# Differences of the inner activations stored with the MLPs' first products, and a list schedule ranked by due times

## The chip, the cores and the metric

The kernel runs on one core of one Trainium2 chip. A core has a matrix engine (TensorE, PE in the profile; PEld is its weight load), VectorE (DVE), ScalarE (ACT), GpSimd (POOL) and SyncE (SP). Here SP issues every DMA. Each engine works through its own instructions in the order in which they were written down, and waits on semaphores of the others. The metric is the device time of one execution in microseconds (us), the median of three runs.

## The reference

Two layers over 1024 tokens of width 1024 in f32, each a mixer and then an MLP:

```
for layer in range(2):
    h = rmsnorm(x, mix_norm[layer])
    x = x + (sliding_window_attention(h) if layer == 0 else hgrn2_recurrence(h))
    h = rmsnorm(x, mlp_norm[layer])
    x = x + square(relu(h @ w_up[layer])) @ w_down[layer]       # inner width 4096
return rmsnorm(x, final_norm)
```

The attention has 16 query heads, 4 key heads, a window of 128 and a sink in the softmax. The recurrence has 8 heads of 128 and chunks of 64, with a forget gate.

## The kernel before

**Tiles.** A tile is 128 features by 512 tokens (`TH`) of f32; two halves of the tokens make `hf` 0 and 1. A product in f32 precision is three matmuls in a faster format (`mm3`): a tile is split into a rounded part and a rest (`split` for activations, `weight_split` for weights), one cast on ACT or DVE and one subtraction on DVE. Tile names show their pool: `wr` raw weights, `wh` and `wl` their two parts, `m` sums of weights, `a` long-lived tiles, `t` short-lived ones, `p` and `q` banks of PSUM, `d` tensors in DRAM. Slots: 60 `a`, 18 `t`, 7 `m`, 5 each of `wr`, `wh`, `wl`, 4 each of `p` and `q`.

**Seven products.** The large matrix products use Strassen's scheme in Winograd's form, once: with the inputs halved in both directions, seven products numbered 1 to 7 take the place of eight. Their operands are the four quarters or sums of them. For activations with quarters 00, 01, 10, 11 (inner half, token half) product 1 takes 00, 2 takes 10, 3 takes 11, 5 takes 01 - 00, 6 takes 11 - (01 - 00), 7 takes 11 - 01, and 4 takes 10 - (11 - (01 - 00)).

**The MLP's first products.** `mlp` first makes the operands of the normalised x (`begin` for the first token half, `finish` for the second, both with splits) and the sums of squares (`weigh`), then calls `pair` for 16 pairs of inner tiles (m and m + 16). A pair runs its seven products of 12 matmuls each into two `q` banks and a `p` bank, reads the banks out, adds, and applies square(relu) to get the four quarters of the inner activations (`square_relu`). `keep` stores each of the four to DRAM by a DMA.

**The MLP's second products.** `down` goes over the 16 inner tiles in passes: products 1 and 5 together, then 6, 7, 4, 2 and 3. For each inner tile `operands` loads the quarters of the weights and of the inner activations that the product needs, makes the sum or difference (`sum_of`, DVE), and splits. The differences of products 5, 6 and 4 build on each other: they live in 16 `a` tiles `T[p]` from pass to pass, and likewise the weights' sums in `S[p]`. Eight activation loads are issued for each inner tile: one for product 1 (its quarter also serves 5), one more for 5, one for 6, two for 7, and one each for 4, 2 and 3.

**The HGRN layer.** `hgrn_constants` makes the lower bounds of the forget gate (small operations on 128 x 8) and the masks (integer operations on 128 x 64). Then `finish` makes the operands of x, `two_first` starts the first head, and eight heads follow: `gates` (Strassen products by `two`) interleaved with the `recurrence` of the head before. `final` makes the last norm.

**What sets the order.** The code above doesn't issue instructions. `Schedule.add` (line 149) notes each operation with its engine or engines, a cost in ns, and what it depends on. `Schedule.order` (line 183) then runs a list schedule: on the engine that is free earliest it takes, of the operations that are ready by its model, the one of the lowest rank, and never idles while one is ready. `LATENCY` is the model's time between engines. A DMA costs its bytes over 320 an ns, at least 650 ns, and lands 2000 ns later. The slots of a pool are given out in the order of the program. The rank is the operation's number in the program less a lead:

```
op.rank = (len(self.ops) - lead, len(self.ops))
```

The lead is 100 operations for the loads and splits of weights (`LEAD`) and for whatever reads a `p` bank (`EVACUATE`), -200 for the last outputs, otherwise 0. Casts can go to ACT or DVE; `better_elsewhere` decides by what is queued. `issue` (line 273) writes the instructions in that order, from one line (341), which is why nearly every row of the profile names L341 and groups are told apart by tiles.

Of the kernel before, what the change touches and what calls it, by code (L numbers as in the profile page):

```python
# [14 lines left out]
ALU = mybir.AluOpType  # L15
AX = mybir.AxisListType

P = 128
T = 1024
# [3 lines left out]
TH = T // NH  # L23
FF = 4096
MT = FF // P
# [93 lines left out]


class Op:
    __slots__ = ("ways", "tail", "bufs", "first", "wait", "ready", "after", "rank", "engine", "form")


ENGINES = ("SP", "PE", "ACT", "DVE", "Pool")
# [7 lines left out]
WEIGH = 1.0  # L133
DRAIN = {"whole": 120.0, "columns": 120.0}
LEAD = 100
EVACUATE = 100
HK = KT // 2


class Schedule:  # L140
# [8 lines left out]
    def add(self, ways, outs, ins, tail=0.0, form=None):  # L149

        op = Op()
        op.ways, op.tail, op.engine, op.form = ways, tail, None, form
        lead = self.lead
        if any(isinstance(v, View) and v.buf.tag == "p" for v in ins):
            lead = max(lead, EVACUATE)
        op.rank, op.ready, op.after, op.first = (len(self.ops) - lead, len(self.ops)), 0.0, [], []
        before, bufs = set(), {}  # L160
        for views, writes in ((ins, False), (outs, True)):
            for v in views:
                if isinstance(v, View):
                    bufs[v.buf] = None
                    before.update(v.buf.conflicts(v.part, writes))
        for views, writes in ((ins, False), (outs, True)):
            for v in views:
                if isinstance(v, View):
                    v.buf.note(op, v.part, writes)
        before.discard(op)  # L170
        op.bufs = list(bufs)
        for b in op.bufs:
            if b.uses == 0:
                op.first.append(b)
                self.tags.setdefault((id(b.pool), b.tag), []).append(b)
            b.uses += 1
            b.users.append(op)
        op.wait = len(before) + len(op.bufs)
        for o in before:
            o.after.append(op)  # L180
        self.ops.append(op)

    def order(self):
        free_at, pending, ready, done, form = {}, {}, {}, [], None
        slots, queue = {}, {}
        for key, bufs in self.tags.items():
# [10 lines left out]
        def give(key):  # L197
            while queue[key] and slots[key]:
                b = queue[key].pop()
                t, b.slot = heapq.heappop(slots[key])  # L200
                for op in b.users:
                    met(op, t)
# [4 lines left out]
                    heapq.heappush(pending.setdefault(e, []), (0.0, op.rank, op))  # L207
        for key in self.tags:
            give(key)
        def better_elsewhere(op, e, t):  # L210
            waiting = sum(o.ways[e][1] for _, o in ready[e] if not o.engine and len(o.ways) == 1)
            for other, (_, cost) in op.ways.items():
                if other != e:
                    ahead = sum(o.ways[other][1] for r, o in ready.get(other, ()) if r < op.rank and not o.engine)
                    if max(t, free_at.get(other, 0.0)) + ahead + cost < t + op.ways[e][1] + WEIGH * waiting:
                        return True
            return False

# [74 lines left out]
class Net:  # L293
# [32 lines left out]
    def a(self, dt=F32, shape=(P, TH)):  # L326
        return self.tile("a", BUFS["a"], shape, dt)
# [171 lines left out]
        return h, self.token_rstd(self.sum_squares([self.x[kt][hf] for kt in range(KT)]))  # L499


    def square_relu(self, m, hf, c, psum):

        r = self.t()
        if psum:
            c, h = straight(c), halves(r)
            self.act(h, c, AF.Relu)
            self.stt(h, c, 0.0, h, ALU.max, ALU.mult)
        else:
            self.stt(r, c, 0.0, c, ALU.max, ALU.mult)  # L510
        self.hid[m, hf] = self.keep(r)

    def gained(self, which, kt, hf):

# [91 lines left out]
    def pair(self, m, x):  # L606

        w = self.strassen_weights(*(self.io["up"][self.layer, i] for i in (m, m + MT // 2)))

        def read(ps):  # L610
            z = self.t()
            self.take(z, ps)
            return z

        main, side, own = self.psum("q"), self.psum("q"), self.psum()
        self.product(main, w[1], x[1], True)
        u1 = read(main)
        self.product(own, w[2], x[2], True)
        self.product(side, w[5], x[5], True)
        p5 = read(side)  # L620
        self.product(main, w[6], x[6], False)
        u2 = read(main)
        self.product(side, w[3], x[3], False)
        self.product(main, w[7], x[7], False)
        u3 = read(main)
        self.product(main, w[4], x[4], False)
        self.add_bank(u1, own)
        self.square_relu(m, 0, u1, False)
        self.add_bank(u2, side)
        self.square_relu(m, 1, u2, False)  # L630
        self.tt("any", p5, p5, u3, ALU.add)
        self.square_relu(m + MT // 2, 1, p5, False)
        self.square_relu(m + MT // 2, 0, main, True)

    def mlp(self, cut):

        x = self.mlp_second()
        for m in range(MT // 2):
            if m == MT // 2 - 2:
                self.r = [self.a() for _ in range(NH)]  # L640
                for hf in range(NH):
                    self.copy(self.r[hf], self.spread(self.square[hf]))
            self.pair(m, x)
        yield from self.down(cut)

    def hidden(self, i, hf, p):
        z = self.t()
        self.dma(z, self.hid[p + i * MT // 2, hf], 4 * P * TH)
        return z

    def operands(self, name, p, T, S, held=False):

        a = lambda i, k: self.raw(self.io["down"][self.layer, k, p, :, i])
        h = lambda i, hf: self.hidden(i, hf, p)

        def sum_of(tile, x, y, alu=ALU.subtract):
            self.tt("any", tile, x, y, alu)
            return tile

        if name == 1:  # L660
            self.corner = a(0, 0), h(0, 0)
            w, x = self.corner
        elif name == 5:
            first, q00 = self.corner
            T[p] = x = sum_of(self.a(), h(0, 1), q00)
            w = sum_of(self.t(tag="m"), a(1, 0), a(1, 1), ALU.add)
        elif name == 6:
            T[p] = x = sum_of(T[p], h(1, 1), T[p])
            w = S[p]
        elif name == 7:  # L670
            x = sum_of(self.t(), h(1, 1), h(0, 1))
            w = sum_of(self.t(tag="m"), a(0, 0), a(1, 0))
        elif name == 4:
            x = sum_of(T[p], h(1, 0), T[p])
            w = a(1, 1)
        elif name == 2:
            w, x = a(0, 1), h(1, 0)
        else:
            x = h(1, 1)
            w = sum_of(S[p], a(0, 1), S[p])  # L680
        got = self.split(w) if held else self.weight_split(w), self.split(x)
        if name == 5:
            S[p] = sum_of(self.a(), w, first)
        return got

    def down(self, cut):
# [2 lines left out]


        n, ahead = MT // 2, 2
        T, S, y = {}, {}, {}
        main = [self.psum("q") for _ in range(HK)]
        side = [self.psum() for m in range(HK)]

# [11 lines left out]
        def run_pass(names, held=0):  # L707
            ws, todo = {}, list(range(n))
            for p in range(n):
                while todo and todo[0] <= p + ahead or (todo and todo[0] >= n - held and p >= n - held - 1):  # L710
                    q = todo.pop(0)
                    for name in names:
                        ws[name, q] = self.operands(name, q, T, S, q >= n - held)
                if p < n - held:
                    products(names, [p], ws, True, n - held - 1)
            return ws
# [551 lines left out]
        self.spill(0)  # L1268

    def hgrn(self, layer):  # L1270
        self.hgrn_constants()
        x, r = self.finish(layer, True), [self.a() for _ in range(NH)]
        begun = [self.two_first(which, 0, x) for which in ((0, 3), (1, 2))]
        self.rs.append(self.token_rstd(self.sum_squares([self.x[kt][1] for kt in range(KT)]), keep=True))
        for y, z in zip(r, self.rs):
            self.copy(y, self.spread(z))
        self.spill(1)
        ys, totals = [[], []], []
        before = iter(())
        for e in range(KT):  # L1280
            got = []
            interleave(self.gates(e, x, self.rs, r, got, [None] * 2 if e else begun), before, 14, 10)
            before = self.recurrence(e, got, totals, ys)
        run(before)
        for y in ys:
            y[:-1] = [self.take_back(kept) for kept in y[:-1]]
        self.hgrn_out(0, ys[0], totals[0])
        self.mlp_first(layer)
        self.hgrn_out(1, ys[1], totals[1])
# [120 lines left out]
```

## Time and profile before

| | us |
|---|---|
| three runs | 2086.87, 2078.36, 2085.83 |
| median | 2085.83 |
| profiled execution, its time | 2076.22 |
| its span, first to last instruction | 2074.4 |
| TensorE busy | 2009.9 |
| VectorE busy | 1809.3 |
| ScalarE busy | 841.8 |
| mean granted TensorE clock | 0.987 of full |

In the order of the span, by the chain of waits and the tiles in use: attention and its projections to about 330 us; the first layer's `pair` products to about 622, its passes of `down` to about 911; the HGRN layer to about 1460; the second layer's pairs to about 1760 and its passes to 2054; the last norm to the end. DMA traffic is heaviest in the passes of `down`.

A row of a group gives the engine, the operation, output and input tiles, the shape and the count; then busy time, mean ns of one, and the engine's idle time just before them with what ended it. A row of the timeline gives the start, the length, the instruction and in brackets the idle time before it with what ended it. A row of a table of stretches gives for each engine its busy time and the number of its instructions, then the granted clock, the share of the DMA engines and GB/s.

### The profile page before, as it was taken

Reading aid. Unit: us, or ns where it says so; the run is one execution under the profiler, and the core shown is the slowest. Engines: PE = TensorE matmul, PEld = TensorE weight load, DVE = VectorE, ACT = ScalarE, POOL = GpSimd, SP = SyncE. Lnnn points to the kernel's source line nnn. Section 1 sums busy time; section 2 is a strip of 40 time slices with the busy share of each in tenths; the row PEclk is TensorE's granted clock in tenths of the full one; section 3 lists DMA queues with packets and bytes.
Section 4 is the critical chain, followed back from the end, with each engine's and each line's share of the span. In section 5 each row is a group of like instructions: output and inputs, shape, how many; then the busy total and the mean of one; then the engine's idle time right before and its main releaser. Section 6 shows DMA issues by size and latency. Waiting matters only on the chain.

```text
span 2074.4 us, 32285 instructions
## 1 busy us (share of the span) xinstructions
PE 2009.9 (97%) x11374; PEld 1722.8 (83%) x11374; DVE 1809.3 (87%) x3598; ACT 841.8 (41%) x1767; POOL 63.8 (3%) x124
## 2 busy tenths in 40 slices
PE   7999999999999999979999999999999999999996
PEld 6878778888888888868888888878788888888886
DVE  8899899777789998899999999879977778999887
ACT  5567765112134334564333333333511124433442
POOL 4030000000000000000100000000000000000001
PEclk9999999999999999999999999999999999999998
DMA  6212363333368877722111111547333337887652
GB/s 209 87 47 81 114 204 126 116 112 122 117 226 291 290 238 251 262 97 72 62 62 57 62 57 62 194 138 243 112 115 116 116 122 237 294 276 241 221 173 82
DMA packets 176450, 316.49 MB, mean 153 GB/s; under 512 B 19744, under 2 KB 23840, under 8 KB 176288
## 3 DMA queue, kind: packets, MB, share of 16 engines
q1 hardware_dynamic: 176288, 314.43, 46.7%
q8 instruction: 89, 1.46, 0.3%
q14 instruction: 73, 0.60, 0.1%
HBM read 250.39 MB, written 63.96 MB: 152 GB/s over the span
## 4 chain that ended last, share of the span: by engine, by line
PE 77%; DVE 14%; DMA 3%; ACT 3%; issue 2%; SPq 0%; DVEq 0%; ACTq 0%
PE q L341 44%; PE p L341 33%; DVE a L341 6%; DVE t L341 4%; DVE m L341 2%; DVE wl L341 2%; DMA wr<-in_down 2%; ACT t L341 1%; ACT a L341 1%; DMA a<-in_x 0%; DMA t<-d 0%; DVE sm L341 0%; DMA t<-in_x 0%; DMA a<-d 0%; ACT wh L341 0%
## 5 line engine op out<-in xcount | busy, mean ns | idle before, releaser
L341 PE MATMUL q<-a,wh 128*128 128x512 f32 x2560 | 763.1, 381 | 10.1 <-ACT t L341 5.9
L341 PE MATMUL p<-a,wh 128*128 128x512 f32 x2336 | 721.4, 388 | 12.9 <-ACT wh L341 11.2
L341 PEld LDWEIGHTS q<-a,wh 128*128 128x128 f32 x2560 | 485.5, 190 | 83.8 <-ACT t L341 8.3
L341 PEld LDWEIGHTS p<-a,wh 128*128 128x128 f32 x2336 | 436.1, 191 | 76.9 <-ACT wh L341 12.0
L341 PE MATMUL q<-a,wl 128*128 128x512 f32 x1280 | 483.1, 381 | 0.3 <-DVE wl L341 0.3
L341 PE MATMUL p<-a,wl 128*128 128x512 f32 x1168 | 447.8, 384 | 0.0
L341 PEld LDWEIGHTS q<-a,wl 128*128 128x128 f32 x1280 | 243.2, 190 | 35.5 <-DVE wl L341 0.7
L341 DVE TENSOR_TENSOR wl<-wr,wh 128x512 fp32r<-128x512 f32 x352 | 240.8, 685 | 11.1 <-ACT wh L341 2.1
L341 PEld LDWEIGHTS p<-a,wl 128*128 128x128 f32 x1168 | 222.7, 191 | 32.6 <-issue 1.2
L341 ACT COPY t<-q 128x512 f32<-128x512 f32 (+2 forms) x201 | 111.5, 561 | 318.0 <-PE q L341 313.4
L341 DVE TENSOR_TENSOR a<-t,a 128x512 fp32r<-128x512 f32 (+1 forms) x294 | 194.9, 683 | 3.6 <-DMA t<-d 3.5
L341 DVE TENSOR_TENSOR wl<-m,wh 128x512 fp32r<-128x512 f32 x256 | 175.0, 685 | 8.2 <-ACT wh L341 1.3
L341 ACT CAST a<-t 128x512 fp32r<-128x512 f32 x198 | 119.5, 617 | 118.7 <-PE q L341 47.5
L341 DVE TENSOR_TENSOR t<-t,t 128x512 f32<-128x512 f32 (+3 forms) x268 | 161.9, 624 | 5.8 <-ACT t L341 2.7
L341 ACT CAST wh<-wr 128x512 fp32r<-128x512 f32 x153 | 94.0, 618 | 160.3 <-PE p L341 89.7
L341 DVE CAST wh<-wr 128x512 fp32r<-128x512 f32 x199 | 85.2, 428 | 81.4 <-PE p L341 51.7
L341 ACT CAST wh<-m 128x512 fp32r<-128x512 f32 x145 | 89.7, 620 | 144.1 <-PE q L341 80.8
L341 DVE TENSOR_TENSOR m<-wr,wr 128x512 f32<-128x512 f32 x160 | 109.6, 686 | 34.9 <-DMA wr<-in_up 18.0
L341 PE MATMUL p<-wh,a 128*128 128x512 f32 x384 | 121.8, 389 | 10.1 <-ACT a L341 8.3
L341 PEld LDWEIGHTS q<-t,t 128*64 128x64 f32 (+1 forms) x2160 | 98.0, 144 | 24.4 <-issue 11.3
L341 PE MATMUL q<-t,t 128*64 128x32 f32 (+2 forms) x2160 | 111.6, 230 | 0.4
L341 ACT CAST a<-a 128x512 fp32r<-128x512 f32 x111 | 67.7, 620 | 79.5 <-DVE a L341 39.5
(117 smaller groups left out, 2082.7 us busy)
## 6 DMA issues: line engine op xcount, KB each, us to landing
t<-d SPq DMA_DIRECT2D x296, 256.0 KB, 4.7
wr<-in_down SPq DMA_DIRECT2D x256, 256.0 KB, 4.0
d<-t SPq DMA_DIRECT2D x180, 256.0 KB, 2.9
wr<-in_up SPq DMA_DIRECT2D x128, 256.0 KB, 2.9
wr<-in_win SPq DMA_DIRECT2D x68, 256.0 KB, 2.8
a<-d SPq DMA_DIRECT2D x60, 256.0 KB, 4.2
wr<-in_wqkv SPq DMA_DIRECT2D x48, 256.0 KB, 2.9
d<-a SPq DMA_DIRECT2D x48, 256.0 KB, 2.5
```

Source lines behind the costliest of these rows:

```text
L341: fn(*[place(a) for a in args], **{k: place(v) for k, v in kw.items()})
```

## The change

Three things change.

The differences of the inner activations are made in `pair` and stored there: seven tensors for each pair instead of four, named by the product that takes them. `operands` loads the one tensor that its product needs, so `T` and its 16 tiles are gone, and the loads for an inner tile go from eight to seven.

`hgrn_constants` is called in the first layer's `mlp`, ahead of its pair 1, instead of at the start of `hgrn`.

The rank becomes a time. `due` first gives every operation a `now`: the TensorE time of all matmuls ahead of it in the program. Then, from the last operation to the first, an operation is due so early that everything that follows from it can still be in time: a matmul at its `now`, any other at most `SLACK` (10 us) after its own `now`. The lead counts as `STEP` (120 ns) each, so 100 are 12 us. `better_elsewhere` now adds, for the other engine too, what is ready there and can run nowhere else.

```diff
@@ class Schedule
+SLACK = 10000.0
+STEP = 120.0
...
-        op.rank, op.ready, op.after, op.first = (len(self.ops) - lead, len(self.ops)), 0.0, [], []
+        op.rank, op.ready, op.after, op.first = lead, 0.0, [], []
...
+    def due(self):
+
+        clock, now = 0.0, []
+        for op in self.ops:
+            now.append(clock)
+            if "PE" in op.ways:
+                clock += op.ways["PE"][1]
+        for i in reversed(range(len(self.ops))):
+            op = self.ops[i]
+            cost = min(c for _, c in op.ways.values())
+            late = now[i] + SLACK
+            for o in op.after:
+                late = min(late, o.due - max(LATENCY[e][w] for e in op.ways for w in o.ways))
+            if "PE" in op.ways:
+                late = min(late, now[i])
+            op.due = late - cost - op.tail
+            op.rank = ((now[i] if "PE" in op.ways else op.due) - STEP * op.rank, i)
+
     def order(self):
+        self.due()
...
+        def load(e):
+            return sum(o.ways[e][1] for _, o in ready.get(e, ()) if not o.engine and len(o.ways) == 1)
+
         def better_elsewhere(op, e, t):
-            waiting = sum(o.ways[e][1] for _, o in ready[e] if not o.engine and len(o.ways) == 1)
+            here = t + op.ways[e][1] + WEIGH * load(e)
...
-                    if max(t, free_at.get(other, 0.0)) + ahead + cost < t + op.ways[e][1] + WEIGH * waiting:
+                    if max(t, free_at.get(other, 0.0)) + ahead + cost + WEIGH * load(other) < here:
@@ pair
+        def kept(name, z):
+            self.hid[name, m] = self.keep(z)
+
         self.add_bank(u1, own)
-        self.square_relu(m, 0, u1, False)
+        h00 = self.square_relu(u1)
+        kept(1, h00)
         self.add_bank(u2, side)
-        self.square_relu(m, 1, u2, False)
+        h01, t5, t6, t4 = self.square_relu(u2), *(self.t() for _ in range(3))
+        self.tt("any", t5, h01, h00, ALU.subtract)
+        kept(5, t5)
         self.tt("any", p5, p5, u3, ALU.add)
-        self.square_relu(m + MT // 2, 1, p5, False)
-        self.square_relu(m + MT // 2, 0, main, True)
+        h11 = self.square_relu(p5)
+        kept(3, h11)
+        self.tt("any", t6, h11, t5, ALU.subtract)
+        kept(6, t6)
+        self.tt("any", h01, h11, h01, ALU.subtract)
+        kept(7, h01)
+        h10 = self.square_relu(main, True)
+        kept(2, h10)
+        self.tt("any", t4, h10, t6, ALU.subtract)
+        kept(4, t4)
@@ mlp
+            if m == 1 and self.layer == 0:
+                self.hgrn_constants()
             self.pair(m, x)
@@ operands
-            self.corner = a(0, 0), h(0, 0)
-            w, x = self.corner
+            w = self.corner = a(0, 0)
         elif name == 5:
-            first, q00 = self.corner
-            T[p] = x = sum_of(self.a(), h(0, 1), q00)
             w = sum_of(self.t(tag="m"), a(1, 0), a(1, 1), ALU.add)
         elif name == 6:
-            T[p] = x = sum_of(T[p], h(1, 1), T[p])
             w = S[p]
         elif name == 7:
-            x = sum_of(self.t(), h(1, 1), h(0, 1))
             w = sum_of(self.t(tag="m"), a(0, 0), a(1, 0))
         elif name == 4:
-            x = sum_of(T[p], h(1, 0), T[p])
             w = a(1, 1)
...
-        got = self.split(w) if held else self.weight_split(w), self.split(x)
+        got = self.split(w) if held else self.weight_split(w), self.split(self.hidden(name, p))
@@ hgrn
-        self.hgrn_constants()
```

More of the change, by code (lines that the diff above doesn't have):

```diff
@@ L121 @@
 class Op:
-    __slots__ = ("ways", "tail", "bufs", "first", "wait", "ready", "after", "rank", "engine", "form")
+    __slots__ = ("ways", "tail", "bufs", "first", "wait", "ready", "after", "rank", "engine", "form", "due")
 ENGINES = ("SP", "PE", "ACT", "DVE", "Pool")
@@ L499, in scaled, with square_relu @@
         return h, self.token_rstd(self.sum_squares([self.x[kt][hf] for kt in range(KT)]))
-    def square_relu(self, m, hf, c, psum):
+    def square_relu(self, c, psum=False):
         r = self.t()
@@ L510, in square_relu @@
             self.stt(r, c, 0.0, c, ALU.max, ALU.mult)
-        self.hid[m, hf] = self.keep(r)
+        return r
     def gained(self, which, kt, hf):
@@ L642, in mlp, with hidden, operands @@
                     self.copy(self.r[hf], self.spread(self.square[hf]))
+            if m == 1 and self.layer == 0:
+                self.hgrn_constants()
             self.pair(m, x)
         yield from self.down(cut)
-    def hidden(self, i, hf, p):
+    def hidden(self, name, p):
         z = self.t()
-        self.dma(z, self.hid[p + i * MT // 2, hf], 4 * P * TH)
+        self.dma(z, self.hid[name, p], 4 * P * TH)
         return z
-    def operands(self, name, p, T, S, held=False):
+    def operands(self, name, p, S, held=False):
         a = lambda i, k: self.raw(self.io["down"][self.layer, k, p, :, i])
-        h = lambda i, hf: self.hidden(i, hf, p)
         def sum_of(tile, x, y, alu=ALU.subtract):
@@ L660, in operands @@
         if name == 1:
-            self.corner = a(0, 0), h(0, 0)
-            w, x = self.corner
+            w = self.corner = a(0, 0)
         elif name == 5:
-            first, q00 = self.corner
-            T[p] = x = sum_of(self.a(), h(0, 1), q00)
             w = sum_of(self.t(tag="m"), a(1, 0), a(1, 1), ALU.add)
         elif name == 6:
-            T[p] = x = sum_of(T[p], h(1, 1), T[p])
             w = S[p]
         elif name == 7:
-            x = sum_of(self.t(), h(1, 1), h(0, 1))
             w = sum_of(self.t(tag="m"), a(0, 0), a(1, 0))
         elif name == 4:
-            x = sum_of(T[p], h(1, 0), T[p])
             w = a(1, 1)
         elif name == 2:
-            w, x = a(0, 1), h(1, 0)
+            w = a(0, 1)
         else:
-            x = h(1, 1)
             w = sum_of(S[p], a(0, 1), S[p])
-        got = self.split(w) if held else self.weight_split(w), self.split(x)
+        got = self.split(w) if held else self.weight_split(w), self.split(self.hidden(name, p))
         if name == 5:
-            S[p] = sum_of(self.a(), w, first)
+            S[p] = sum_of(self.a(), w, self.corner)
         return got
@@ L691, in down @@
         n, ahead = MT // 2, 2
-        T, S, y = {}, {}, {}
+        S, y = {}, {}
         main = [self.psum("q") for _ in range(HK)]
@@ L712, in run_pass @@
                     for name in names:
-                        ws[name, q] = self.operands(name, q, T, S, q >= n - held)
+                        ws[name, q] = self.operands(name, q, S, q >= n - held)
                 if p < n - held:
```

## The prediction

> **What bounds the kernel now.** I read the page first, then the table of stretches, then TensorE's own timeline for its stalls, then the chain of waits around each. The profiled execution took 2076.22 us for a span of 2074.4, so 1.8 lies around the span; it is 9.6 us below the median of the three runs (2085.83). The sum is made against 2076.22 and the same difference is then taken off the median.
>
> ```profile
> span 2074.4 us, 32285 instructions
> PE 2009.9 (97%) x11374; PEld 1722.8 (83%) x11374; DVE 1809.3 (87%) x3598; ACT 841.8 (41%) x1767; POOL 63.8 (3%) x124
> ...
> 400.00:580.00 180.00, 180.00 (x832) 156.88 (x831) 138.34 (x247) 35.03 (x61) 0.00 (x0) 1.00 0.36 116
> ...
> 622.00:705.00 83.00, 82.99 (x377) 72.40 (x378) 77.13 (x129) 34.87 (x60) 0.00 (x0) 0.98 0.89 292
> 746.00:787.00 41.00, 40.80 (x189) 35.42 (x188) 38.44 (x66) 16.38 (x30) 0.00 (x0) 1.00 0.91 307
> 868.00:922.00 54.00, 52.90 (x250) 46.06 (x248) 53.98 (x123) 38.10 (x70) 0.36 (x2) 1.00 0.46 159
> ...
> 703.39 33.47 PE q L341 x155
> ```
>
> The columns of a stretch are its length, the busy time of PE, weight load, DVE, ACT and POOL, the granted clock, the DMA share and GB/s. TensorE is idle for 2074.4 - 2009.9 = 64.5 us. Inside the MLPs' first products (400 to 580) it never stops. The chain's piece of 155 matmuls in 33.47 us gives 0.216 us a matmul, so no order of the others can make these stretches shorter. What can be won lies in the stalls, which are few:
>
> ```profile
> 8.27 0.80 PE L341 MATMUL p<-wh,a 128*128 128x512 f32 x1 [8.27 <-ACT a L341]
> ...
> 278.21 1.09 PE L341 MATMUL q<-c,m 128*128 128x128 f32 x4 [4.31 <-DVE m L341]
> 622.01 0.70 PE L341 MATMUL q<-a,wh 128*128 128x512 f32 x2 [1.87 <-DVE t L341]
> 934.02 1.22 PE L341 MATMUL p<-a,wh 128*128 128x512 f32 x2 [10.14 <-ACT wh L341]
> 1385.76 1.13 PE L341 MATMUL q<-t,c 128*128 128x512 f32 x2 [2.34 <-DVE t L341]
> 1466.88 1.22 PE L341 MATMUL q<-a,wh 128*128 128x512 f32 x2 [2.15 <-ACT t L341]
> 1760.27 0.70 PE L341 MATMUL q<-a,wh 128*128 128x512 f32 x2 [1.48 <-DVE t L341]
> 1925.86 0.70 PE L341 MATMUL q<-a,wh 128*128 128x512 f32 x2 [3.01 <-ACT t L341]
> ...
> 925.00:930.00 5.00, 0.00 (x0) 0.00 (x0) 5.00 (x9) 4.81 (x10) 0.00 (x0) 0.66 0.00 0
> 930.00:935.00 5.00, 0.97 (x2) 0.50 (x2) 5.00 (x9) 2.41 (x5) 0.00 (x0) 0.50 0.08 24
> 935.00:940.00 5.00, 5.00 (x12) 3.86 (x12) 5.00 (x12) 0.94 (x3) 0.00 (x0) 0.50 0.64 186
> 1927.00:1930.00 3.00, 3.00 (x9) 2.35 (x8) 3.00 (x6) 1.83 (x4) 0.00 (x0) 0.50 1.00 339
> ...
> 934.02 9.54 PE p L341 x28
> ...
> 1466.88 10.73 PE q L341 x35
> ...
> 625.02 3.26 PE q L341 x12
> ```
>
> The number in brackets is the idle time before the matmul. Each stall also costs afterwards, since the granted clock falls to 0.50: the 28 matmuls after 934.02 took 9.54 us where 28 x 0.216 = 6.05 would do, 3.5 lost; the 35 after 1466.88 lost 10.73 - 7.56 = 3.2; the 12 at 625.02 lost 0.67; from 1927 to 1930, 9 ran where 14 fit, 1.1 lost. At the largest stall DVE is busy without a gap (5.00 of 5.00, three times): the entry to the HGRN layer is bound by VectorE.
>
> **The change part by part.** First, 4 subtractions for each of 16 inner tiles and 2 layers, 128 in all, leave the second products and are made in `pair`. One is a row like this, read beside the stores and loads of 256 KB:
>
> ```profile
> L341 DVE TENSOR_TENSOR t<-t,t 128x512 f32<-128x512 f32 x10 | 6.8, 684 | 0.0
> ...
> d<-t SPq DMA_DIRECT2D x180, 256.0 KB, 2.9
> ...
> t<-d SPq DMA_DIRECT2D x296, 256.0 KB, 4.7
> ```
>
> The number of subtractions is unchanged. 400 to 580 holds ten of those `t<-t,t`, one a pair, so ten pairs of 18 us; DVE is busy 13.8 of each 18, ACT 3.5. Four more make 13.8 + 4 x 0.684 = 16.6. It fits, hidden behind matmuls: cost 0. With that cover gone, what DVE needs beyond 18 us would count 32 times. The stores go from 4 to 7 for each pair (96 more), the loads from 8 to 7 for each inner tile (32 fewer). Three more stores put 0.79 MB into 18 us, 44 GB/s above the 116 of the row: cost 0, with 292 reached elsewhere. Behind a waiting store SP holds later weight loads; 0.36 of DMA time in use leaves that room.
>
> In the second products DVE loses 16 x 0.684 = 11 us in each of four passes. It was 38.44 of 41 busy in the pass of product 7 (746 to 787), which also loads least freely: four loads for 12 matmuls (2.59 us), 1.05 MB, 405 GB/s wanted where the row shows 307. With three loads 304 are wanted, which that row about reaches. The 16 tiles that kept the running differences through the passes come free for loading ahead. The 3.01 + 1.1 us at 1925.86, at the end of that pass, should go. At the starts of the passes (1.87 + 0.67 and 1.48) the wait is for the last pair's bank, and reading it out gets a later due time under the change; I leave these. Term: -4, between -8 (all of them) and +4 (the two starts double).
>
> Second, the masks of the HGRN layer move to the first layer's pairs, where DVE has time:
>
> ```profile
> L341 DVE TENSOR_SCALAR t<-t 128x64 int32<-128x64 int32 x13 | 2.3, 180 | 0.0
> L341 DVE TENSOR_TENSOR c<-c,t 128x64 int32<-128x64 int32 x6 | 1.3, 212 | 0.0
> L341 DVE TENSOR_SCALAR c<-t 128x64 int32<-128x64 int32 (+1 forms) x7 | 1.2, 181 | 0.0
> L341 DVE TENSOR_SCALAR c<-c 128x64 int32<-128x64 int32 x6 | 1.1, 180 | 0.0
> ```
>
> These 32 operations run between 860 and 936 in the stretch that DVE bounds: 5.9 us busy; overlapped at their ends they take less, by a step of about 0.1 us some 3.4. I take 3.4 off the stall at 934.
>
> Third, the rank. Before, an operation's place in the program less a lead; after, the time at which it must start for its matmul to come at its place on a TensorE that never waits. Engines still take any ready operation, so the rank decides only where several are ready: the stretches that DVE fills. At 934 the program's order makes all the differences of x (four groups of 4 subtractions, five splits of 4) before the second weights of the first head. By due time the operands of product 5 (x5: 8 operations, weight: 2) come before those of products 6, 7 and 4. Step by step: the two first products of each pair run to about 924; product 5 wants 10 DVE operations of some 0.6 us (nine fill the 5.00 from 925 to 930), product 6 ten more, 7 and 4 as many, each against 2.6 us of matmuls. DVE stays the bound, but 5 and 3 fill holes that are now one hole of 10.14. The sum of squares, 7 additions or 4.2 us, gets an early due time too, because its small matmuls stand ahead of product 5, and this eats part of it. Of 10.14 + 3.5 = 13.6, I take 3.4 from the masks and 5.6 from the order: -9, between -13.6 and +4 (the additions put ahead, nothing gained).
>
> At 1466.88 the same kind of entry loses 2.15, and 3.2 after: -2, between -5.4 and +4. The stalls at 278 and 1385 are chains of dependent operations (softmax, a reciprocal root) that rank can shorten little: -1 each, between -3 and +2.
>
> The start is where the deadline rule is worse:
>
> ```profile
> 1.18 0.42 SPq L341 DMA_DIRECT2D c<-in_par  x1
> ...
> 2.11 4.51 SPq L341 DMA_DIRECT2D a<-in_x  x8
> ...
> 8.00:12.00 4.00, 3.73 (x9) 3.01 (x10) 3.68 (x9) 4.00 (x8) 0.00 (x0) 1.00 1.05 397
> 12.00:17.00 5.00, 3.47 (x17) 2.69 (x15) 5.00 (x10) 5.00 (x10) 0.00 (x0) 1.00 0.90 308
> ```
>
> Gains (`par`) are loaded second now, and the first matmul runs at 8.27. Under due times five weight loads (lead 12 us) and the eight x loads (wanted early by the sum of squares) come before `par`, which only the scaling needs. That is 13 x 0.26 = 3.4 MB ahead of it, 11 us at 308 GB/s, and near 3 us more to land: par at 14, the first matmul at 15. But until 17 only 9 + 17 = 26 matmuls ran, 5.6 us, so today's start is worth a start at 11.4. Term: +3.5, between 0 and +6.5 (15 - 8.3).
>
> The balance between ACT and DVE now counts the other engine's queue as well, which sends casts from a full DVE to an ACT at 41%; no stall hangs on it alone: 0, between -4 and +4.
>
> Sum: -4 - 9 - 2 - 1 - 1 + 3.5 = -13.5. That is 2062.7 for the profiled execution, and 2085.83 - 13.5 = 2072 for the median.
>
> The Trainium skill's page "TensorE: Matmul & The Clock Gate" (section "Part 1: The HAM clock gate") says that the clock halves after an idle window of about 3.4 us and recovers after as long a busy one. Against it, the clock here was 0.50 after 1.87 us of idling; the measurement decides. By the page only the stalls at 934 and 278 would cost afterwards, and the sum would be about -12.4, without the 1.1 after 1925.86.
>
> **The rivals.** *The stalls move, none goes* (20%): DVE's total is the same, and where it fills a stretch only the masks' 3.4 and the 4 of the second products come off, less 3.5 at the start: -4, so 2081. For it: DVE at 53.98 of 54 us. Against it: one hole of 10 us with a cold clock is the worst shape.
>
> *All of it closes* (13%): 13.6 at 934, 5.4 at 1466, 6.6 at 278 and 1385, 8.1 in the second products, less 3.5: -30, so 2056. For it: DVE gets 11 us free in each of four passes, and ACT has room. Against it: chains at 278 and 1385.
>
> *The order is the old one* (7%): the cap of 10 us and the same leads give nearly the program's order, start included; masks and second products remain: -7.4, so 2078.
>
> *Slower* (15%): the sum of squares goes ahead of the operands at the three entries (about 330, 920, 1460): 7 additions of 0.6 us, then the cold clock, 4.2 + 3.5 = 7.7 each. Nothing is gained there, 23 is added, with +3.5 at the start and -6 from the rest: +20, so 2106. It decides from 0.8 us at each entry, (6 - 3.5) / 3. For it: at 330 DVE is full without a stall today. Against it: the additions become ready early, one a token tile.
>
> **How the numbers follow.** The forecast has 45%. About what a measurement of this kernel tells from no change is 0.5%, 10.4 us. The forecast's own range is 2062 to 2084; of its 45 points I put 37 beyond 0.5% faster and 8 within. Faster: 37 + 13 = 50%. Same: 8 + 20 + 7 = 35%. Slower: 15%. The range reaches from just below the rival where all closes, 2055, to halfway into the slower one, 2093.
>
> **What would show it.** Right: the stall at 934 split into pieces of under 4 us, 5 us less in all; no stall near 1925; DVE near 16.6 of 18 us in a pair with TensorE still at 100%; the first matmul later than 12 us. Wrong: TensorE under 99% in the pairs; a stall of over 3 us near 335; the first matmul still at 8.3 (then the due times don't order SP as I read them).

## The result and the profile after

The kernel after takes 2048.04 us (median; 2045.51 to 2050.98), the kernel before 2082.22: a ratio of 0.9837, 95% interval 0.9811 to 0.9862. A second measurement gave 0.9845 (0.9822 to 0.9868). The profiled execution took 2047.32 us for a span of 2045.4, 29.0 less than the span before. The medians lie 34.2 apart; the profiled execution of the kernel before (2076.22) was shorter than all four of its timed runs (2078.36 at the least). The medians of the second measurement, taken beside the kernel before, differ by 29.6. The account below goes by the profiles. The forecast was 13.5 less, and its range ended at 2055.

First the page of the kernel after: span, busy times, chain, two kinds of DMA.

```profile
span 2045.4 us, 32633 instructions
PE 1997.1 (98%) x11374; PEld 1717.4 (84%) x11374; DVE 1793.4 (88%) x3551; ACT 868.8 (42%) x1815; POOL 62.8 (3%) x124
...
PE 81%; DVE 8%; DMA 5%; ACT 3%; issue 2%; SPq 0%; DVEq 0%; ACTq 0%
...
d<-t SPq DMA_DIRECT2D x276, 256.0 KB, 2.7
t<-d SPq DMA_DIRECT2D x264, 256.0 KB, 4.6
```

TensorE is idle for 2045.4 - 1997.1 = 48.3 us, 16.2 less than before. The other 12.8 of the 29.0 us are busy time: the same 11374 matmuls took 1997.1 instead of 2009.9, because fewer of them ran at half clock: the mean granted clock is 0.994, before 0.987, so the clock withheld is worth 0.006 x 2045.4 = 12.3 us of full speed against 0.013 x 2074.4 = 27.0, a part of it while TensorE stood idle. In sum the stalls that closed returned nearly twice their own length. The stores and loads are as the edit says: 96 more, 32 fewer.

Then TensorE's own timeline at the places of the old stalls.

```profile
14.64 0.80 PE L365 MATMUL p<-wh,a 128*128 128x512 f32 x1 [14.64 <-ACT a L365]
...
330.16 0.70 PE L365 MATMUL q<-a,wh 128*128 128x512 f32 x2 [1.36 <-ACT t L365]
...
621.61 0.67 PE L365 MATMUL q<-a,wh 128*128 128x512 f32 x2 [0.78 <-DVE t L365]
...
929.14 0.79 PE L365 MATMUL p<-a,wh 128*128 128x512 f32 x1 [6.19 <-DVE a L365]
...
1370.49 1.10 PE L365 MATMUL q<-t,c 128*128 128x512 f32 x2
...
1447.28 0.96 PE L365 MATMUL q<-a,wh 128*128 128x512 f32 x3 [0.96 <-ACT wh L365]
```

The first matmul comes 6.4 us later. The stall of 10.14 at the entry to the HGRN layer is one of 6.19. At its exit the matmuls `q<-t,c`, which waited 2.34 us at 1385.76 before, run at 1370.49 with no bracket, so without idling. Of the 0.83 and 2.15 at the second MLP's entry 0.96 is left. Nothing over 0.7 us is left near 278, where 4.31 stood, nor where 1.48 and 3.01 stood in the second layer's passes. The 1.36 at 330.16, at the entry to the first MLP, is new, with two of about 0.5 near 350; the kernel before has none over 0.6 there.

The table of stretches of the kernel after (columns as in the prediction):

```profile
400.00:580.00 180.00, 180.00 (x832) 156.60 (x831) 150.53 (x256) 52.35 (x92) 0.00 (x0) 1.00 0.48 160
...
747.00:788.00 41.00, 41.00 (x192) 35.90 (x191) 33.55 (x58) 14.61 (x26) 0.00 (x0) 1.00 0.77 253
...
1360.00:1390.00 30.00, 29.64 (x155) 25.52 (x154) 27.74 (x58) 19.87 (x34) 0.00 (x0) 1.00 0.72 235
1440.00:1457.00 17.00, 16.04 (x79) 13.67 (x78) 17.00 (x31) 12.67 (x25) 0.00 (x0) 1.00 0.16 48
...
1895.00:1915.00 20.00, 20.00 (x94) 17.50 (x94) 17.77 (x31) 9.79 (x17) 0.00 (x0) 1.00 0.87 300
```

In the pairs TensorE stays at 180.00 of 180. DVE is busy 15.05 us of 18, ACT 5.2 (13.8 and 3.5 before): four subtractions came and about three casts a pair went to ACT.

The time of each stage, difference to the kernel before. Both traces have the same 9214 matmuls on whole 128-row tiles; the start of the k-th in one is set against that of the k-th in the other. Stages end at k = 1750 (in the first pairs), 4000 (last pass of the first layer), 4300, 5950, 6400, 6600 and 8600.

| stage | after | predicted |
|---|---|---|
| start, attention, first MLP entry | +0.3 | +3.5 - 1 |
| first pairs and passes | -2.7 | -4 with the second layer's |
| HGRN entry | -4.1 | -9 |
| HGRN heads | -2.7 | 0 |
| HGRN exit | -7.7 | -1 |
| second MLP entry | -5.9 | -2 |
| second pairs and passes | -6.1 | (above) |
| last norm | -0.1 | 0 |
| sum | -29.0 | -13.5 |

A second trace of the same kernel after has -29.6 in all, and in one stage differs by 1.2 us (-5.3 at the HGRN entry), in the others by 0.5 at most. So a difference of about 1 us between two kernels at that entry says nothing.

### The profile page after: what moved, and what is told of

The parts are those of the page before. It is cut to its first block, busy times and chain, and to the rows that moved or that the text cites. A ratio compares the mean times of both kernels' runs of the same rounds, so it can differ in the third digit from the quotient of the medians.

```text
span 2045.4 us, 32633 instructions
## 1 busy us (share of the span) xinstructions
PE 1997.1 (98%) x11374; PEld 1717.4 (84%) x11374; DVE 1793.4 (88%) x3551; ACT 868.8 (42%) x1815; POOL 62.8 (3%) x124
## 4 chain that ended last, share of the span: by engine, by line
PE 81%; DVE 8%; DMA 5%; ACT 3%; issue 2%; SPq 0%; DVEq 0%; ACTq 0%
PE q L365 45%; PE p L365 36%; DVE t L365 3%; DVE a L365 3%; DMA wr<-in_down 2%; DMA t<-d 2%; DVE wl L365 1%; ACT t L365 1%; DVE m L365 1%; ACT a L365 1%; ACT wh L365 1%; DMA a<-in_x 1%; ACT m L365 0%; SPq L365 0%; DMA wr<-in_win 0%
## 5 line engine op out<-in xcount | busy, mean ns | idle before, releaser
L365 ACT CAST a<-t 128x512 fp32r<-128x512 f32 x287 | 173.8, 618 | 287.5 <-PE q L365 135.9
L365 DVE TENSOR_TENSOR t<-t,t 128x512 f32<-128x512 f32 (+3 forms) x364 | 223.5, 638 | 4.7 <-ACT t L365 3.2
L365 DVE TENSOR_TENSOR a<-t,a 128x512 fp32r<-128x512 f32 (+1 forms) x326 | 216.3, 683 | 7.3 <-ACT a L365 6.8
L365 ACT CAST wh<-m 128x512 fp32r<-128x512 f32 x174 | 107.8, 620 | 264.7 <-PE q L365 192.3
L365 DVE TENSOR_TENSOR wl<-m,wh 128x512 fp32r<-128x512 f32 x256 | 175.5, 685 | 12.8 <-ACT wh L365 7.5
L365 ACT CAST wh<-wr 128x512 fp32r<-128x512 f32 x175 | 108.0, 618 | 181.0 <-PE p L365 100.1
L365 DVE CAST wh<-wr 128x512 fp32r<-128x512 f32 x177 | 75.7, 428 | 67.1 <-PE p L365 34.5
L365 PEld LDWEIGHTS p<-wh,a 128*128 128x128 f32 x384 | 72.4, 192 | 25.0 <-ACT a L365 14.6
```

What stands on the lines that cost most here:

```text
L365: fn(*[place(a) for a in args], **{k: place(v) for k, v in kw.items()})
```

## The experiments

The theories. Main: the gain is the order of DVE's work by due times, and the moves only relieve the second products. Rivals: the moves bring it; the new balance brings it; what matters is only that rank is a time, not that due times are counted back from the matmuls. On the stall left at 929: that the second sum of squares stands ahead of product 5's operands (S), or that the cap of 10 us ranks work too early there (K). No run has both moves and the new balance under the old rank.

**The parts alone.** The old schedule with both moves; the new schedule (rank and balance) with neither; the differences alone; and the kernel after with the old balance.

```diff
 differences alone: old schedule, pair and operands as after, and
@@ hgrn
+        self.hgrn_constants()
 old balance:
-            here = t + op.ways[e][1] + WEIGH * load(e)
+            waiting = sum(o.ways[e][1] for _, o in ready[e] if not o.engine and len(o.ways) == 1)
...
-                    if max(t, free_at.get(other, 0.0)) + ahead + cost + WEIGH * load(other) < here:
+                    if max(t, free_at.get(other, 0.0)) + ahead + cost < t + op.ways[e][1] + WEIGH * waiting:
```

> Old rank and old balance, both moves (differences made in the pairs, masks in the first layer's pairs). Theory A (the due times pay most, at the entries of the stages): only the passes of the second products and the masks gain, 4 to 10 us, ratio to the kernel before 0.995 to 0.998; the first matmul at 8.3 as before; the stalls near 1385 and 1467 of before stay. Theory B (the work taken off VectorE pays most): 20 us or more, ratio 0.991 or below.

> Due times and new balance, neither move. Theory A: 18 to 24 us off, ratio 0.988 to 0.991, with the first matmul at 14.6 and the holes near 278, 1385 and 1467 of before closed. Theory B: 10 us or less, ratio 0.995 or above.

> Old rank and old balance, differences moved, masks left where they were. Against the run with both moves this gives the masks' price: by the prediction 3.4 us more than with both moves, all of it at the entry to the HGRN layer. If the masks are hidden there, no difference beyond 1 us.

> The changed kernel with the old choice between ScalarE and VectorE. Theory A (the rank carries it): within 4 us of the changed kernel, ratio to before 0.982 to 0.987. The rival (the new choice frees VectorE and carries much of the unforeseen gain): 10 us or more above the changed kernel, ratio 0.988 or above.

The last column here and below is the start of the last matmul in the profiled execution, less that of the kernel before.

| | us | ratio to before, interval | trace |
|---|---|---|---|
| both moves, old schedule | 2066.73 | 0.9950 (0.9935 to 0.9966) | -9.5 |
| new schedule, no move | 2056.41 | 0.9900 (0.9873 to 0.9927) | -25.2 |
| differences alone | 2068.46 | 0.9954 (0.9940 to 0.9969) | -8.5 |
| after, old balance | 2056.05 | 0.9897 (0.9876 to 0.9917) | -19.7 |

The schedule carries most of the gain, the moves about a third of it. The parts can be put on one after another: the moves give 9.5 us in the trace, the new rank on top of them 10.2 more (to -19.7), the new balance on top of both 9.3 more (to -29.0), so each is about a third. Whether moves and schedule overlap can't be told: by the traces 9.5 + 25.2 is 34.7 and not 29.0, by the ratios 0.50% + 1.00% is 1.50% against 1.63%. TensorE's timeline with the moves and the old schedule shows what they don't touch:

```profile
278.12 0.66 PE L341 MATMUL q<-c,m 128*128 128x128 f32 x2 [4.31 <-DVE m L341]
893.49 0.79 PE L341 MATMUL p<-a,wh 128*128 128x512 f32 x1 [6.11 <-ACT wh L341]
937.65 0.70 PE L341 MATMUL p<-a,wh 128*128 128x512 f32 x2 [3.42 <-ACT t L341]
1385.26 1.77 PE L341 MATMUL q<-t,c 128*128 128x512 f32 x2 [2.35 <-DVE t L341]
```

The stalls at 278 and 1385 are as before. In place of that at 934 there are two, 6.11 + 3.42 = 9.53 for 10.14, though the masks are gone from there; the entry as a whole gains 0.0. The stalls at 622, 1760 and 1926 do go with the moves: the second pairs and passes gain 5.9 by them alone, and 2.2 with the schedule alone.

**Due times counted back, or only a place in time.** Every operation ranked by its `now` less its lead, without `due`:

```diff
-            op.rank = ((now[i] if "PE" in op.ways else op.due) - STEP * op.rank, i)
+            op.rank = (now[i] - STEP * op.rank, i)
```

> The changed kernel with the rank of every operation its place in TensorE time less the lead; nothing is counted back from what follows it. Theory L (looking back along the chains pays): the holes near 278 and 1385 of before come back, 12 us or more lost against the changed kernel, ratio to before 0.989 or above. Theory U (it is the unit, time in place of a count of operations): within 4 us of the changed kernel. In both the first matmul comes back to 8 to 9 us, since the gains go first again.

2056.17 us, ratio 0.9904 (0.9870 to 0.9938); the trace has -22.2. So counting back is worth 6.8 of the 29.0 us by the trace, 0.67% by the ratios, and a rank that is only a place in time, with the moves and the new balance, keeps the rest. How much of that rest is the time and how much the balance, no run tells. TensorE's timeline of this kernel:

```profile
8.60 0.80 PE L365 MATMUL p<-wh,a 128*128 128x512 f32 x1 [8.60 <-ACT a L365]
276.07 0.79 PE L365 MATMUL p<-a,wh 128*128 128x512 f32 x1 [3.29 <-DVE a L365]
926.43 1.17 PE L365 MATMUL p<-a,wh 128*128 128x512 f32 x2 [4.20 <-ACT t L365]
1371.57 0.70 PE L365 MATMUL q<-t,c 128*128 128x512 f32 x1 [2.35 <-DVE t L365]
1452.59 0.80 PE L365 MATMUL q<-a,wh 128*128 128x512 f32 x1 [5.06 <-ACT t L365]
```

The late start is gone and the HGRN entry is even better (-7.7 against -4.1). But a stall at 276 and the one at the HGRN exit are back, and one of 5.06 stands at the second MLP's entry. Over all kernels the exit splits cleanly: -7.7 or -7.8 wherever due times are counted back, -1.5 here, between 0.0 and -0.3 with the old rank. VectorE's timeline shows why. The reciprocal root that the exit waits for is a row of tiny operations on `sm` tiles. Before:

```profile
1379.33 0.18 DVE L341 RECIPROCAL sm<-sm 128x4 f32<-128x4 f32 x1 [0.27 <-ACT sm L341]
...
1381.62 0.68 DVE L341 TENSOR_TENSOR wl<-wr,wh 128x512 fp32r<-128x512 f32 x1
1382.22 0.68 DVE L341 TENSOR_TENSOR a<-t,a 128x512 fp32r<-128x512 f32 x1
1382.83 0.15 DVE L341 TENSOR_TENSOR sm<-sm,sm 128x4 f32<-128x4 f32 x1
1382.90 0.68 DVE L341 TENSOR_TENSOR wl<-wr,wh 128x512 fp32r<-128x512 f32 x1
1383.50 0.16 DVE L341 TENSOR_SCALAR sm<-sm 128x4 f32<-128x4 f32 x1
1383.57 0.68 DVE L341 TENSOR_TENSOR wl<-wr,wh 128x512 fp32r<-128x512 f32 x1
...
1384.25 0.68 DVE L341 TENSOR_TENSOR wl<-wr,wh 128x512 fp32r<-128x512 f32 x1
1384.85 0.86 DVE L341 TENSOR_SCALAR t<-c,sm 128x128 f32<-128x128 f32 x4
```

After:

```profile
1365.83 0.18 DVE L365 RECIPROCAL sm<-sm 128x4 f32<-128x4 f32 x1 [0.27 <-ACT sm L365]
...
1368.13 0.16 DVE L365 TENSOR_SCALAR sm<-sm 128x4 f32<-128x4 f32 x1
1368.20 0.69 DVE L365 TENSOR_TENSOR wl<-wr,wh 128x512 fp32r<-128x512 f32 x1
1368.80 0.15 DVE L365 TENSOR_TENSOR sm<-sm,sm 128x4 f32<-128x4 f32 x1
...
1369.48 0.87 DVE L365 TENSOR_SCALAR t<-c,sm 128x128 f32<-128x128 f32 x4
```

And with the place in time alone:

```profile
1365.12 0.18 DVE L365 RECIPROCAL sm<-sm 128x4 f32<-128x4 f32 x1 [0.27 <-ACT sm L365]
...
1370.65 0.86 DVE L365 TENSOR_SCALAR t<-c,sm 128x128 f32<-128x128 f32 x4
```

From the reciprocal to the scaling it took 5.52 us before, 3.65 after and 5.53 here. The tiny operations themselves need 0.15 to 0.18 us each. Between them VectorE runs full-size ones, with one gap of 0.35 to 0.43 us: four weight splits (`wl<-wr,wh`) before, four here, one after, and in all three kernels a cast and three others. The splits start 0.6 us after one another, so three fewer are 1.8 of the 1.87 us. It was a queue, not a chain.

**The cap, the sum of squares, the start.** Three single edits to the kernel after:

```diff
-SLACK = 10000.0
+SLACK = 30000.0
 a second kernel, around the second token_rstd(sum_squares(...)) in hgrn:
+        self.s.lead = -100
         self.rs.append(self.token_rstd(self.sum_squares([self.x[kt][1] for kt in range(KT)]), keep=True))
+        self.s.lead = 0
 a third kernel, around the DMA of par:
+        self.s.lead = 200
...
+        self.s.lead = 0
```

> The changed kernel with the cap on due times at 30 us instead of 10. Theory K: the stall at 929 goes below 3 us, since the operands of products 6, 7 and 4 become due later than those of 5; 3 to 6 us won there. Theory S: it stays above 4 us. Stores wait up to 20 us longer in rank, which could cost slots: a loss of up to 5 us elsewhere is possible.

> The changed kernel with the sum of squares of the second token half at the entry to the HGRN layer put 12 us back in rank. Theory S (the sum goes ahead of the operands of product 5 and makes the stall of 6.19 us at 929): the stall falls below 3 us, and 3 to 6 us with the cold clock are won. Theory K (the cap of 10 us gives the operands of products 5, 6, 7 and 4 the same due time, so that VectorE makes the differences of all before the rests of the first): the stall stays above 4 us.

> The changed kernel with the load of the gains (par) given a lead of 24 us, so that it is the first load. The prediction's reading of the start: the first matmul comes back to 8 to 10 us, and 3 to 4 us are won in all (the 3.8 that the changed kernel is behind at its 250th matmul). Rival: the weights and x loads would keep it waiting anyway, under 1 us won.

The cap of 30 us gives 2061.71, ratio 0.9921 (0.9899 to 0.9944), 15.5 us more in the trace than with 10, of which 7.3 are lost up to the pairs and 2.6 at the HGRN entry: it is not a larger cap that mends the entry (8.79 us of stall there), so K falls. With the second sum of squares put later the entry gains 9.3 instead of 4.1; the two traces of the kernel after and those of the two kernels with the gains first and with the masks put back have 4.1 to 5.8 there, so the edit is worth 3.5 to 5.2. This bears out S. VectorE's timeline of the kernel after, ahead of 929.14, and then that of this kernel:

```profile
922.39 6.10 DVE L365 TENSOR_TENSOR t<-t,t 128x512 f32<-128x512 f32 x10
928.41 0.68 DVE L365 TENSOR_TENSOR a<-t,a 128x512 fp32r<-128x512 f32 x1
```

```profile
922.45 2.48 DVE L365 TENSOR_TENSOR t<-t,t 128x512 f32<-128x512 f32 x4
924.86 7.30 DVE L365 TENSOR_TENSOR a<-t,a 128x512 fp32r<-128x512 f32 x12
```

After, ten subtractions and additions stand ahead of the rest `a<-t,a` for which TensorE waits; with the sum later it is four. The stall is 2.82 us instead of 6.19. With the gains read in first the first matmul starts at 8.79 instead of 14.64, and 4.9 us of that last to the pairs (-4.6 against +0.3). As times, neither edit alone can be told from the kernel after: 2043.11 and 2042.90, ratios 0.9838 (0.9800 to 0.9877) and 0.9839 (0.9801 to 0.9877).

**Both edits together, the kernel after beside them, the balance alone, the masks put back.** The first has both edits above. The third is the kernel before with the new `load` and `better_elsewhere`. The last is the kernel after with

```diff
@@ mlp
-            if m == 1 and self.layer == 0:
-                self.hgrn_constants()
@@ hgrn
+        self.hgrn_constants()
```

> The kernel after with both mends: gains read in 24 us ahead of their due time, and the HGRN entry's second sum of squares put 12 us later. If each mended its own place, the gains of the two alone add up: about 4.6 us at the start and 3.5 to 5 at the HGRN entry, 8 to 10 less than the kernel after on the same chip, ratio to the kernel before 0.979 to 0.981. If the earlier start only moves work that then waits elsewhere, 3 to 5 less, as for either alone.

> The kernel after unchanged, beside the kernel before on the same chip as the two mends: a ratio of 0.981 to 0.986 is expected from its first measurement (0.9837). It is the measure for what the mends are worth.

> The kernel before with one change, the new balance between ACT and DVE; rank and both moves as before. If the balance is worth the 9 us that the kernel after lost when it was taken out (0.5 us for each HGRN head, the rest at the entry of the HGRN layer and in the second layer's passes), whatever the order: 2067 to 2072, ratio 0.993 to 0.997, with the gain spread over the heads. If it works only together with the due times (which fill DVE's queue with ready operations that the balance then sees): no change, ratio 0.998 to 1.002, and the heads as long as before.

> The kernel after with the masks and lower bounds of the HGRN layer made where the kernel before makes them, at that layer's start. If the move is worth the 3.4 us that the prediction gave it (DVE bounds the entry), the stall near 929 grows by about that: 2050 to 2052, ratio 0.986 to 0.988. If the due times let these operations slip behind the ones that the first products wait for, or into idle ends, as the run with the differences alone beside the one with both moves suggests (1.7 us between them, with no change at that stall): within 1 us of the kernel after, ratio 0.983 to 0.985.

| | us | ratio to before, interval | trace |
|---|---|---|---|
| both edits | 2038.27 | 0.9801 (0.9777 to 0.9824) | -37.2 |
| after, again | 2046.92 | 0.9845 (0.9822 to 0.9868) | -29.6 |
| balance alone | 2072.99 | 0.9982 (0.9964 to 1.0001) | -2.7 |
| masks put back | 2046.26 | 0.9847 (0.9831 to 0.9863) | -31.2 |

Both edits together beat both kernels: 8.65 us under the kernel after on the same chip, with 4.5 us more gained up to the pairs (-4.2 against +0.3) and 6.5 at the HGRN entry (-10.6 against -4.1); 3.3 of it is lost again in the second layer's pairs and passes (-2.8 against -6.1), where a stall of 1.99 us stands at 1726.30, at the start of the passes, with a granted clock of 0.56 from 1727 to 1730. TensorE's timeline at the start and at the HGRN entry:

```profile
8.54 0.80 PE L367 MATMUL p<-wh,a 128*128 128x512 f32 x1 [8.54 <-ACT a L367]
919.65 0.48 PE L367 MATMUL p<-a,wh 128*128 128x512 f32 x1 [2.64 <-DVE a L367]
923.94 0.48 PE L367 MATMUL p<-a,wh 128*128 128x512 f32 x1 [1.64 <-ACT t L367]
```

The balance is worth 9.3 us inside the kernel after (-29.0 against -19.7), and no measurable difference alone. Alone it shortens the heads by 2.8 as it does there, but opens other holes, for example (TensorE's timeline of that kernel)

```profile
786.49 0.70 PE L344 MATMUL q<-a,wh 128*128 128x512 f32 x2 [4.24 <-ACT t L344]
```

at which TensorE waits for ACT. Why the due times avoid that hole was not tested.

The masks are worth nothing where they were moved from. In the kernel before they ran between 890 and 905. Two of the groups of that stretch:

```profile
L341 DVE TENSOR_SCALAR c<-t 128x64 int32<-128x64 int32 x6 | 1.1, 181 | 0.0
L341 DVE TENSOR_TENSOR t<-t,t 128x64 int32<-128x64 int32 x1 | 0.2, 211 | 0.0
```

The other integer groups lie there too, and none after 905, while TensorE works on to 923.9. So they ended 18 us before the stall at 934 began. Put back in the kernel after, where they run between 897 and 940, they cost nothing that can be measured.

## Why the prediction was wrong

The direction was right; the size was missed by 15.5 us, in several terms:

- **"The stalls at 278 and 1385 are chains of dependent operations (softmax, a reciprocal root) that rank can shorten little: -1 each."** This step failed, and cost most. The exit gave -7.7. Between k = 1000 and 1350, around 278, the trace gains 7.6; the kernel with both edits, which starts as early as before, gains 7.4 there. At the exit the runs show a queue of ready weight splits ahead of tiny operations. At 278 that is not shown: VectorE is full there before and after. What differs is TensorE's order. Before, the matmuls `q<-c,m` at 278.21 follow those at 273.27 with no other between; after, 29 others stand between those at 275.65 and 280.55, so TensorE has work while it waits. Which of the new ranks brought that was not tested; without counting back 3.29 us of stall is there again. The stretch 270 to 280, before and then after:

```profile
270.00:280.00 10.00, 5.40 (x34) 3.56 (x33) 10.00 (x22) 10.00 (x32) 0.00 (x0) 0.91 0.65 202
```

```profile
270.00:280.00 10.00, 10.00 (x65) 8.17 (x65) 9.92 (x23) 10.00 (x32) 0.00 (x0) 1.00 0.53 177
```

  The step behind it failed too, that the rank decides only in "the stretches that DVE fills": at the exit DVE is busy 22.59 of 30 us, and three splits at the wrong moment are enough. And no slow clock was counted at either place. A stretch of the kernel before around the exit has it at 0.89:

```profile
1370.00:1400.00 30.00, 25.86 (x135) 21.97 (x136) 22.59 (x55) 16.18 (x30) 0.00 (x0) 0.89 0.53 176
```

  The idle part is 30 - 25.86 = 4.1, of which 0.4 is left after (29.64 of 30 in the row from 1360), the slow clock 0.11 x 30 = 3.3, all gone after: together 7.0 of the 7.7.
- **HGRN entry, -9: measured -4.1.** The 3.4 for the masks was wrong, since they ran before the stretch that matters; of the 5.6 for the order the sum of squares ate 3.5 to 5.2, where the prediction said only that it "eats part of it". With the sum put later, and no other edit at the entry, the term is -9.3: the due times can give what was forecast, and the kernel after doesn't get it.
- **Second products, -4: measured -8.8** with both layers (-2.7 and -6.1), beyond the bound of -8. The stall at 1925.86 went, as forecast: the row 1895 to 1915, which holds its place, shows TensorE at 20.00 of 20, and the row 747 to 788, around the first layer's pass of product 7, at 41.00 of 41. But there the DMA engines move 253 GB/s and not the 304 worked out, so the pass did without that rate; which loads came ahead of it was not followed. The two starts of passes, put at nothing, gained too: nothing over 0.6 is left of 1.48, and 0.78 of 1.87. With the moves and the old schedule both are gone; with the due times beside the moves other traces have up to 2.07 us at the first start (masks put back) and 1.99 at the second (both edits). Why the moves close them, the runs don't settle: those moves also free 16 `a` tiles.
- **Entry at 1466, -2: measured -5.9**, just past its bound. It falls to 0.0 without counting back, so it is the order that closes it. (The moves alone have -2.8 there with stalls as before, 0.70 and 2.15, but with the clock at 1.00.)
- **The balance, 0: measured -9.3** inside the kernel after, over twice the bound of 4; 2.7 of it are the HGRN heads, which the sum had at 0. The run with the balance alone gains nothing measurable; the error was to price a part of the schedule by itself.
- **The start, +3.5: measured +3.8** at the 250th matmul, the first matmul at 14.64 where 15 was forecast. It was then made up at 278, which the sum did not foresee (-2.3 at k = 1475), and 2.6 of that is lost again at the entry to the first MLP, in the stall of 1.36 at 330.16 and two of about 0.5 near 350, so that +0.3 is left at the pairs.
- **The pairs, 0: measured 0.** DVE took 15.05 of 18 us, not 16.6, as about three casts a pair went to ACT. The new balance is not the cause: from 400 to 580 DVE is busy 150.63 us in the kernel after with the old balance, and 150.78 with the moves and the old schedule. The old choice already sends casts away from a fuller DVE, which the 16.6 left out.

The rival where all of it closes (-30, given 13%) is near the total, but not for its reasons: it had 13.6 at the HGRN entry, of which 4.1 came, and 6.6 at 278 and 1385, which returned over twice that (7.6 + 7.7). That the total came near it is luck. The slower rival's mechanism is shown at one of its three places: the sum of squares stands ahead of the operands at 922, and putting it later returns 3.5 to 5.2 us. At the other two entries the stalls are 1.36 us (330.16) and 0.96 (1447.28); at the first of them 2.6 us are lost, and whether the sum of squares does that was not tested.

Of the signs named: no stall near 1925, and the first matmul later than 12 us, came. The stall at 934 did not split into pieces under 4 us; it is one of 6.19, which is the mark of the sum of squares.

## What to carry to other kernels

Before a stall is called a chain of dependent operations, list what the engine ran between the links: full-size operations among tiny ones point to a queue, which a rank counted back from the matmul that waits can close, as at the exit here. A rank by due times ranks everything that has an early consumer, sums of squares and input loads too, so look at what it pulls ahead of the critical operands, and give those a later or earlier lead by hand. Price a stall with the slow matmuls that follow it, and the parts of a scheduler together, not one by one.

## What the runs showed of the hardware

The clock did not follow the length of a stall alone. The kernel before had 0.50 from 623 to 626, after 1.87 us of idling. In the kernel with both edits, stalls of 2.64 and 1.64 us within 5 us left it at 1.00, and in the one with the sum later 2.82 us brought 0.50. Stretches of the former and the latter:

```profile
919.00:923.00 4.00, 2.64 (x11) 1.96 (x11) 4.00 (x7) 3.36 (x7) 0.00 (x0) 1.00 0.00 0
923.00:927.00 4.00, 3.06 (x14) 2.68 (x15) 4.00 (x11) 1.17 (x2) 0.00 (x0) 1.00 0.00 0
```

```profile
925.00:928.00 3.00, 2.41 (x6) 1.96 (x7) 3.00 (x6) 3.00 (x7) 0.00 (x0) 0.50 0.01 3
928.00:931.00 3.00, 3.00 (x9) 2.37 (x8) 3.00 (x6) 1.21 (x3) 0.00 (x0) 0.50 0.00 0
```

One stall in two kernels is the plainest pair. At the second MLP's entry the kernel before has stalls of 0.83 and 2.15 us, and then 0.50 from 1468 to 1471. The kernel with both moves and the old schedule has 0.70 and 2.15 us there, the latter at 1465.92, and then:

```profile
1466.00:1469.00 3.00, 3.00 (x14) 2.65 (x15) 3.00 (x6) 3.00 (x7) 0.00 (x0) 1.00 0.00 0
```

And with the cap of 30 us a stall of 1.29 us at 335.01, close to eight matmuls of one column each, was followed by 0.51 from 336.6 to 340. So in these traces a stall between 1.29 and 2.82 us may or may not cost a cold stretch. The Trainium skill's page "TensorE: Matmul & The Clock Gate" (section "Part 1: The HAM clock gate") says that the window in which activity is counted runs freely and is not started by the kernel. That agrees with different outcomes for like stalls; its about 3.4 us of idling for the drop does not agree with the 1.87 us here.
